# Values of the two dilated attention groups: projected in token order and re-sorted through DRAM

## The chip, the cores and the metric

The kernel runs on one core of a Trainium2 chip. The metric is the device time of one execution, in microseconds, as a median of several runs; less is better. The core has a matrix engine (TensorE, PE in the profile; its weight loads are listed apart as PEld), VectorE (DVE), ScalarE (ACT), GpSimd (POOL) and SyncE (SP), which here only issues transfers. Each engine works through its own queue in order. All operands of the matrix products are split into a high and a low part, and three products (high x high, high x low, low x high) stand for one product in full precision.

## The reference

One decoder layer over 1024 tokens of 1024 features: token mixing, a norm, a mixture of experts, a second norm. Token mixing projects the input once and hands the columns to three mixers. The one that matters here is the dilated mixer, with three groups of four heads of 64, of dilation 1, 4 and 16:

```python
def to_sub(t):
    return t.reshape(Bsz, Ls, dil, H, hd).transpose(0, 2, 1, 3, 4).reshape(Bsz * dil, Ls, H, hd)
qs, ks, vs = to_sub(q), to_sub(k), to_sub(v)
s = banded_logits(qs[:, :, :, None], ks, bias[:, None], steps)
...
o = jnp.einsum('bnhgqk,bnkhd->bnqhgd', (e / l).astype(v.dtype), band_blocks(vs, n))
```

So in a group of dilation d a token attends to tokens of its own residue class modulo d, and queries, keys and values are put in the order of the classes first. The outputs of the three groups are merged with weights from their softmax denominators. Beside it run a sliding-window mixer and a latent-attention mixer, and the output projection joins all three.

## The kernel before, in words

The part up to the routing is written as tasks. A task (line 170) is a few matrix products with the steps of other engines behind them, with estimated costs. The class Order (line 196) holds lists of tasks, the streams, in the order of the string STREAMS (line 55), and issues, one after another, the task or step that could start first by its estimates; among nearly equal ones, the earlier stream wins. Within a stream the order is fixed. Buffers are tokens: a task takes them by name when it is issued ("mm" for six PSUM banks, "ph" for four staging tiles, "v" for one large tile of values, "qk" for six query and key tiles), and gives them back after its products or steps. Stream P holds the projections, Q the scores and softmax, T the transposes of the probabilities, V the products with the values.

The projection is a list of units (line 875). A unit "cols" (cols_tasks, line 571; qk_tasks, line 607) makes 128 columns of queries or keys with the weights stationary and 512 tokens moving. A unit "v" (v_tasks, line 626) makes values key-major: x is stationary (128 features x 128 tokens), the weights move (256 columns for groups 1 and 2, 416 for group 0, which takes the values of the sliding window and the shared latent key along). Per block of 128 tokens it runs 8 feature tiles x 3 products = 24 matmuls, in two tasks. For groups 1 and 2 the block is a block of the order by residue classes, so its 128 tokens lie 4 or 8 apart in the tile of x (dilation 16 is run as 8, with every second distance masked out):

```python
                r, m = divmod(b, npc)
                sl = slice(m * P * dil + r, (m + 1) * P * dil, dil)
```

The result goes from PSUM by two steps, a cast on ACT and a subtraction on DVE (split2, line 370), straight into the tile of values "vB1" or "vB2" in its place [128 keys, block, pair, (high low low high), 64]. There is one buffer "v" for the values of all groups: a group's values can be made only when the products of the group before have read theirs.

Weights are loaded by SP in chunks of 256 KB into three raw buffers up to two units ahead (wload, line 514), and split by ACT and DVE in steps that every projection task carries (wsteps, line 523), with at most eight split chunks alive.

The order in stream P is: three latent units, then the values of group 1 mixed piece by piece with the latent keys and values (which are staged in "ph" tiles and stored to DRAM, mla_units, line 1240), then the first queries of group 1 mixed with the latent rotary part and latent queries, then keys and queries of group 1, and then for group 2 queries, keys, values, queries, keys, and the same for group 0. The attention of a group (banded, line 682) runs beside it as streams Q, T and V. The products with the values start with line 803. Outputs and statistics of groups 1 and 2 are written to DRAM by POOL (lines 999, 1062 to 1069), and so are the bias tables (row_tasks, line 462), which SP loads back (line 494).

Of the kernel before, what the change touches and what calls it, by code (L numbers as in the profile page):

```python
# [20 lines left out]
P = 128  # L21
# [33 lines left out]
STREAMS = 'VTGRLQPlE'  # L55
# [114 lines left out]
class Task:  # L170
    """Matrix products that belong together, with the work of the other engines that follows them.

    fn: a generator issues the products up to its first yield, then one step of post at a time; a plain
    function issues everything at once.  pe and post: weights of the work on the engines ("T": a transfer),
    which steer the order of issue: for a generator a list of steps (engine, weight[, step it follows]), for
    a function a list of chains of them.  alloc, free: named buffers that the task takes, and gives back
    after its products ("pe"), after a step of its post work ("at": number of steps -> buffers) or after all of it.
    """
# [10 lines left out]
class Buf:  # L189
    """A buffer of a kind, taken by one task and given back by another."""  # L190
# [5 lines left out]
class Order:  # L196
    """Issues tasks of several streams, and the steps of each, by the time at which they could start."""
# [12 lines left out]
    def take(self, kind):  # L210
        """The slot of the next buffer of this kind that the task at hand has taken."""
        return self.task.got[kind].pop(0)
# [86 lines left out]
    def run(self, streams):  # L299
        """streams: lists of tasks, the ones to prefer first."""  # L300
# [22 lines left out]
class MixedPool:  # L323
    """A pool whose tags have their own numbers of buffers."""
# [16 lines left out]
class K:  # L341
# [13 lines left out]
    def buf(self, kind, shape, dt, name):  # L355
        """A tile in the buffer of this kind that the task at hand has taken."""
        pool = {"mm": self.ps, "o": self.ps, "qk": self.qk, "ot": self.ob, "sq": self.pp}[kind]
        return pool.tile(shape, dt, name=name, tag="%s%d" % (kind, self.ord.take(kind)))

    def split(self, h, l, src, scale=None):  # L360
        """src = h + l (times scale), both exactly what a one-pass product reads."""
        nc = self.nc
        if scale is None:
            nc.scalar.copy(h, src)
            nc.vector.tensor_tensor(l, src, h.bitcast(F32), ALU.subtract)
        else:
            nc.scalar.activation(h, src, AF.Copy, scale=scale)
            nc.vector.scalar_tensor_tensor(l, src, scale, h.bitcast(F32), ALU.mult, ALU.subtract)

    def split2(self, h, l, src, scale=None, low=None):  # L370
        """The two steps of a split."""
# [11 lines left out]
    def mm3(self, out, st, mv, start, stop, **kw):  # L383
        """out += st.T @ mv for operands split as (high, low)."""
# [5 lines left out]
    # ---------------------------------------------------------------- set up  # L390
    def setup(self):
# [14 lines left out]
        self.d_v = dt("d_v", [8, P, 2, 512])  # L406
        self.d_kr = dt("d_kr", [2, 32, T])
# [11 lines left out]
    def startup(self):  # L419
        """Loads and splits x, with the first weights; returns stand-ins for when each part is there."""  # L420
# [41 lines left out]
    def row_tasks(self, g):  # L462
        """Per head -bias over the distance, +BIG where masked, replicated so that a sheared read is a table."""
# [33 lines left out]
    # ------------------------------------------------------- input projections  # L497
    def weights_of(self, unit):
        """The unit's weights in chunks of up to 2 KB: (source, shape, gains)."""
# [23 lines left out]
    def wsteps(self, u):  # L523
        """Splits the next weights of the units after u, as far as their buffers are free; then loads ahead."""
# [46 lines left out]
    def cols_tasks(self, u, unit, begin, evac, alloc=(), post=None, first=False, deps=()):  # L571
        """128 columns of the projection, d-major.  begin(): takes the destination; evac(half, psum)."""
# [34 lines left out]
    def qk_tasks(self, u, unit, cell, bufs):  # L607
        """q or k of two heads, split, tokens ordered by residue class; cell receives (high, low)."""
# [17 lines left out]
    def v_tasks(self, u, unit, begin, dests, alloc):  # L626
        """v, key-major: per 128-key block [pair, (H L | L H), 64] into dests() (column, pairs, tile)."""
        nc = self.nc
        _, key, dil = unit
        n = VCOLS[key]  # L630
        per = 2 if n == 256 else 1
        npc = 8 // dil if dil > 1 else 8
# [3 lines left out]
        def piece(b, part):  # L636
            if dil == 1:
                sl = slice(b * P, (b + 1) * P)
            else:
                r, m = divmod(b, npc)  # L640
                sl = slice(m * P * dil + r, (m + 1) * P * dil, dil)

            def fn():
                if b == 0 and part == 0:
                    begin()
# [10 lines left out]
                if part == 1:  # L656
# [11 lines left out]
        for b in range(8):  # L668
            for part in range(2):
# [3 lines left out]
                post = post + [("A", 0.48), ("D", 0.6)]  # L673
                if part == 0:
                    mm = Buf("mm")
                tasks.append(Task(piece(b, part), pe, post,
                                  alloc=([mm] if part == 0 else []) + (list(alloc) if b + part == 0 else []),
                                  free=[mm] if part else ()))
        return tasks

    # --------------------------------------------------------- banded attention
    def banded(self, name, q, k, v, tb, heads, chain, negm, l, init, out, deps, ends, ot):
        """Attention of the two heads of a tile over chains of 128-query blocks; out(bank, psum).

        q, k, v, tb, negm, l: functions, called when issued.  Returns tasks for the three streams;
        ends: (buffers given back by the last scores, by the last products)."""
# [5 lines left out]
        for b0 in range(0, 8, 2):  # L692
# [41 lines left out]
            for js in (ready[:2], ready[2:]):  # L734
# [5 lines left out]
                for h in range(2):  # L740
# [14 lines left out]
                    # the score tiles of the step before are no longer read  # L755
# [45 lines left out]
    def pv(self, out, v, p, first):  # L801
        """The halves of out add up to += v.T @ p.  v: ([a | b], high), a and b high and low or reversed; p: (high, low)."""
# [3 lines left out]
    def head_of(self, v, h):  # L806
        """([a | b], high) of a head of [keys, 4, 64]."""
        return v[:, 2 * h:2 * h + 2, :].rearrange("p i d -> p (i d)"), v[:, 3 * h]

    def unfold(self, dst, ps, h):  # L810
        """Adds up the halves of a bank of outputs of head h of a pair, to its tokens; two steps."""
# [8 lines left out]
    def spread_tasks(self, name, f, hf, use, deps, free, post=(), ps_tag="mm"):  # L820
        """Factors f() [token, block, 2 heads] of four blocks as a psum tile [2 heads x 64, 512 tokens]: use(it)."""
# [24 lines left out]
    # ----------------------------------------------------------- all mixers  # L846
    def phase_attention(self):
# [29 lines left out]
        for gi, (g, dil) in enumerate(((1, 4), (2, 8), (0, 1))):  # L877
# [4 lines left out]
            if g == 1:  # L882
                units[6 + 1] = u[0]
                u = [u[1]] + u[3:]
            units += u
# [12 lines left out]
        cells, st, tabs, vt = {}, {}, {}, {}  # L898
# [4 lines left out]
        def mixed(a, b):  # L903
            """a with b spread over it."""
            return [t for i, x in enumerate(a) for t in b[i * len(b) // len(a):(i + 1) * len(b) // len(a)] + [x]]

        for ui, u in enumerate(units):
# [6 lines left out]
            elif u[0] == "v":  # L914
# [9 lines left out]
                tk = self.v_tasks(ui, u, begin, dests, ["v", "va"] if nm == "B0" else ["v"])  # L924
                if nm == "B1":
                    early["v"] = list(tk)
                else:
                    Pt += tk
                last["v" + nm] = tk[-1]
                if nm == "B0":  # L930
# [76 lines left out]
        # sliding window with sinks  # L1007
# [32 lines left out]
        mix_end = V[-1]  # L1040
        return Pt, Q, TT, V, L, krt

    def scale_tasks(self, nm, cell, f, deps, dst, ot):
        """The outputs of a pair times its factors, and away."""
# [27 lines left out]
    def merge_tasks(self, pr, cell, st, deps, ot):  # L1072
        """The three groups' outputs weighted by exp(m_g - M) / sum."""
# [44 lines left out]
    def latent_unit(self, ui, u, name, n, lat, first, final):  # L1118
        """Compressed q or kv, normalised (the gains go into the weights), split, d-major."""
# [82 lines left out]
    def key_rope_tasks(self, kr, dep):  # L1202
        """The shared decoupled key, rotated token-major, then d-major and split."""
# [35 lines left out]
    # ------------------------------------------------------ latent attention  # L1239
    def mla_units(self, u, which, lat):  # L1240
        """Keys, queries, values of latent attention from the compressed ones, split, into DRAM."""
# [23 lines left out]
        if which == "v":  # L1265
# [19 lines left out]
            # the compressed keys and values are no longer read  # L1285
# [59 lines left out]
    def mla_open(self):  # L1345
        """Takes over from the projections."""
# [38 lines left out]
    def kq_load(self, n):  # L1385
        """Keys and queries of head n: [96, (k high, k low, q high, q low), tokens]."""
# [12 lines left out]
    def mla_tasks(self, deps, tr):  # L1399
        """Tasks of the pairs of heads."""  # L1400
# [20 lines left out]
    def dense(self, n, qp, ld, vt, tr, cell):  # L1421
        """Causal attention of a head for the query blocks 2 qp and 2 qp + 1."""
# [111 lines left out]
    # ------------------------------------ output projection, norm, routing  # L1534
    def wo_tasks(self, part, deps):
        """Weights of the output projection, four tiles of input rows, split."""
# [22 lines left out]
    def part_tasks(self, deps):  # L1559
        """alpha x + the part of the output projection that comes from the banded mixers."""  # L1560
# [51 lines left out]
    def out_tasks(self, qdeps, deps, wdeps, pend):  # L1612
        """qdeps: all scores of latent attention; deps: all of latent attention; wdeps: the weights."""
# [201 lines left out]
    def place_tasks(self, b, m, deps, c_, cell):  # L1815
        """Experts of the tokens of m blocks from b on, and the tokens' places there."""
# [92 lines left out]
    def slot_parts(self, pool, b, n=0, eng=None, nb=5):  # L1909
        """One-hot positions, and (2 token + k + 1) at the expert, of the tokens of block b."""  # L1910
# [14 lines left out]
    def slot_index(self, tabps, idx, tok):  # L1925
        """Row 2 token + k of the outputs and token of each slot; -1 where the slot is free."""
# [14 lines left out]
    def gates(self):  # L1941
        """Softmax over the chosen two, times the group's probability."""
# [15 lines left out]
    def phase_mixers(self):  # L1958
        """All mixers, output projection, norm and routing, as streams of tasks."""
        self.wos = {}  # L1960
        Pt, Q, TT, V, L, krt = self.phase_attention()
# [6 lines left out]
        m = dict(E=E, V=[V + V2], R=R, T=[TT + T2], Q=[Q + Q2], L=[L], P=[Pt + [tr] + part + Y], l=[ld, pl, wl, xl], G=G)  # L1968
        self.ord.run([s for k in STREAMS for s in m[k]])

    # --------------------------------------------------------------- experts
# [10 lines left out]
    def chunk(self, shape, i, nm):  # L1982
        """Buffer i for a chunk of weights."""
# [426 lines left out]
```

## Time and profile before

| what | value |
|---|---|
| median of three runs | 1147.3 us |
| the three runs | 1146.27, 1147.3, 1148.0 us |
| span of the profiled execution | 1146.1 us |
| mean granted TensorE clock in it | 0.957 |
| PE busy, PEld busy | 1045.4 us, 877.4 us |
| DVE, ACT, POOL busy | 768.1, 690.1, 205.7 us |
| moved by DMA | 222.65 MB, 194 GB/s on the mean |

The page gives the span, from the first to the last instruction, and no other time for the profiled execution; the runs' times lie about 1 us above it. Rows of a view of instructions read: line, engine, operation, output tile <- input tiles, shape, count, then busy time in us and the mean of one in ns, then the idle time before them with what ended it. Rows of the timeline read: start and duration in us, engine, line, operation, tiles; idle time before it stands in brackets. Records of neighbouring matmuls overlap, so the pace of PE is read from the distance of their starts. Rows by stage read: from:to in us, length, then busy time and number of instructions of PE, PEld, DVE, ACT and POOL, the granted clock, the share of DMA time and GB/s. The number behind a DMA's size is the median time from issue to landing. The value projections have the output tile psv_B, the attention outputs o_B, scores S_B, transposed probabilities pt_B; the numbers of groups and buffers are left out of the names.

### The profile page before, as it was taken

What the parts mean: (1) busy time and instruction counts of PE and PEld (TensorE: products, weight loads), DVE (VectorE), ACT (ScalarE), POOL (GpSimd) and SP (SyncE); (2) the same over time, 40 slices, a digit from 0 to 9 for tenths busy, and PEclk for the clock granted to TensorE, in tenths of its full rate; (3) what the DMA queues carried; (4) which work ended last, traced back from release to release, by engine and by line L of the source; (5) the groups of instructions that cost most, each with busy time, mean ns of one, the idle gap of its engine ahead of it and who ended that gap; (6) DMA issues with size and microseconds to landing.
All of it is one profiled execution on the core that took longest, in us unless ns stands there. A gap on an engine that the chain in (4) does not pass through costs nothing. (4 is left out here: it accounts for less than half of the span.)

```text
span 1146.1 us, 16350 instructions
## 1 busy us (share of the span) xinstructions
PE 1045.4 (91%) x5611; PEld 877.4 (77%) x5611; DVE 768.1 (67%) x1623; ACT 690.1 (60%) x1442; POOL 205.7 (18%) x219
## 2 busy tenths in 40 slices
PE   7999999999999999889999988948999999999941
PEld 5898778899879888779888867747788777777710
DVE  4443645523443566787877647787899999999758
ACT  4323255422543465687956534457999888888754
POOL 1000000200110011000310123453233222221126
PEclk9999999999989999999999989878999999999976
DMA  7135452200250311947555286447999999999273
GB/s 261 51 140 188 172 175 83 86 10 30 72 132 1 97 45 49 262 109 215 154 155 143 79 285 229 142 184 271 370 379 381 396 377 382 376 379 366 96 314 135
DMA packets 67382, 222.65 MB, mean 194 GB/s; under 512 B 12532, under 2 KB 20148, under 8 KB 53728
## 3 DMA queue, kind: packets, MB, share of 16 engines
q1 hardware_dynamic: 53328, 187.98, 46.5%
q0 software_dynamic: 13968, 33.60, 8.4%
q8 instruction: 45, 0.74, 0.3%
q14 instruction: 41, 0.34, 0.1%
HBM read 187.62 MB, written 53.82 MB: 211 GB/s over the span
## 5 line engine op out<-in xcount | busy, mean ns | idle before, releaser
L2129 DVE TENSOR_TENSOR el<-er,eh 128x1024 fp32r<-128x1024 f32 x188 | 225.9, 1220 | 26.3 <-ACT eh L2127 25.5
L2127 ACT CAST eh<-er 128x1024 fp32r<-128x1024 f32 x188 | 193.7, 1057 | 2.4 <-PE gu L388 2.0
L386 PE MATMUL gu<-eh,xh 128*128 128x512 f32 x256 | 103.8, 405 | 0.0
L387 PE MATMUL gu<-el,xh 128*128 128x512 f32 x256 | 103.7, 405 | 0.0
L388 PE MATMUL gu<-eh,xl 128*128 128x512 f32 x256 | 101.0, 395 | 0.0
L386 PE MATMUL psv_B<-wh,xH 128*128 128x256 f32 (+1 forms) x192 | 73.3, 382 | 2.2 <-ACT wh L374 1.7
L387 PE MATMUL psv_B<-wl,xH 128*128 128x256 f32 (+1 forms) x192 | 74.4, 387 | 0.4 <-DVE wl L376 0.3
L388 PE MATMUL psv_B<-wh,xL 128*128 128x256 f32 (+1 forms) x192 | 74.1, 386 | 0.0
L1456 ACT ACTIVATE PC<-PC,mnC 128x512 f32<-128x512 f32 (+3 forms) x96 | 58.6, 616 | 19.9 <-DVE mnC L1450 19.7
L1973 POOL DMA_INDIRECT xg<-d_x,tok x32 | 37.6, 1174 | 150.2 <-PE gx L2144 142.9
L387 PEld LDWEIGHTS gu<-el,xh 128*128 128x128 f32 x256 | 48.1, 188 | 20.4 <-DVE el L2129 10.3
L386 PEld LDWEIGHTS psv_B<-wh,xH 128*128 128x128 f32 x192 | 54.7, 285 | 4.6 <-ACT wh L374 2.5
L717 ACT ACTIVATE P_B<-P_B,negm_B 128x128 f32<-128x128 f32 (+1 forms) x96 | 42.4, 442 | 23.2 <-DVE negm_B L713 23.0
L1978 POOL DMA_INDIRECT d_y<-y,idx x32 | 39.4, 1232 | 92.7 <-ACT y L2182 74.8
L387 PEld LDWEIGHTS psv_B<-wl,xH 128*128 128x128 f32 x192 | 54.8, 285 | 1.6 <-DVE wl L376 1.5
L376 DVE TENSOR_TENSOR vB<-psv_B,vB 128x256 fp32r<-128x256 f32 x24 | 10.2, 424 | 68.2 <-ACT vB L374 68.2
L386 PEld LDWEIGHTS gu<-eh,xh 128*128 128x128 f32 x256 | 48.1, 188 | 10.2
L388 PEld LDWEIGHTS psv_B<-wh,xL 128*128 128x128 f32 x192 | 55.2, 287 | 0.1
L388 PEld LDWEIGHTS gu<-eh,xl 128*128 128x128 f32 x256 | 48.1, 188 | 9.2
L376 DVE TENSOR_TENSOR plC<-ptC,phC 128x512 fp32r<-128x512 f32 (+1 forms) x80 | 46.7, 630 | 11.6 <-ACT phC L374 11.1
L386 PE MATMUL y<-eh,hh 128*128 128x512 f32 x128 | 53.1, 415 | 0.7 <-ACT hh L374 0.7
L374 ACT CAST vB<-psv_B 128x256 fp32r<-128x256 f32 x24 | 8.9, 372 | 72.3 <-PE psv_B L388 72.3
(432 smaller groups left out, 2987.2 us busy)
## 6 DMA issues: line engine op xcount, KB each, us to landing
er<-in_w_gu SPq DMA_DIRECT2D x63, 1024.0 KB, 15.2
er<-in_w_dn SPq DMA_DIRECT2D x32, 1024.0 KB, 13.0
wr<-in_w_qk SPq DMA_DIRECT2D x36, 256.0 KB, 3.9
fy<-d_y SPq DMA_DIRECT2D x7, 1024.0 KB, 11.7
kqs<-d_k SPq DMA_DIRECT2D x16, 256.0 KB, 11.0
kqs<-d_qn SPq DMA_DIRECT2D x16, 256.0 KB, 5.0
vC<-d_v SPq DMA_DIRECT2D x8, 512.0 KB, 9.1
xr<-in_x SPq DMA_DIRECT2D x16, 256.0 KB, 6.4
```

The lines of the kernel that those rows point to most:

```text
L374: nc.scalar.copy(h, src)
L376: (low or nc.vector).tensor_tensor(l, src, h.bitcast(F32), ALU.subtract)
L386: nc.tensor.matmul(out, st[0], mv[0], start=start, stop=False, **kw)
L387: nc.tensor.matmul(out, st[0], mv[1], start=False, stop=False, **kw)
L388: nc.tensor.matmul(out, st[1], mv[0], start=False, stop=stop, **kw)
L717: nc.scalar.activation(p[:, i, :w], p[:, i, :w], AF.Exp, bias=negm()[:, b, hh:hh + 1], scale=-1.0, accum_out=l()[:, b, hh:hh + 1])
L1456: nc.scalar.activation(pt[:, c:c + w], pt[:, c:c + w], AF.Exp, bias=mn[:, 1:2], scale=-1.0, accum_out=sm["l"][:, b, n, i:i + 1])
L1973: self.nc.gpsimd.indirect_dma_start(out=xg, out_offset=None, in_=self.d_x1, in_offset=bass.IndirectOffsetOnAxis(ap=tok.bitcast(U32), axis= ...
L1978: return self.nc.gpsimd.indirect_dma_start(out=self.d_y, out_offset=bass.IndirectOffsetOnAxis(ap=idx.bitcast(U32), axis=0), in_=y, in_offs ...
L2127: nc.scalar.copy(hi[:, s], t[:, s])
L2129: nc.vector.tensor_tensor(lo[:, s], t[:, s], hi[:, s].bitcast(F32), ALU.subtract)
```

## The change

The values of groups 1 and 2 are now projected in blocks of 128 consecutive tokens, as those of group 0 already were. The split goes to a staging tile out of the four "ph" tiles, and SP stores it as 128 rows of 2 KB to a new DRAM tensor. When all eight blocks of a group are stored and the buffer "v" is free, POOL loads the values back, one DMA for each residue class (4 for group 1, 8 for group 2), with every dil-th row. This load is a task of a new stream N, placed ahead of P. The products with the values depend on it. The values of group 2 move ahead of that group's first queries and keys in stream P; the projection of groups 1 and 2 takes no "v" buffer any more, and the first task of group 0's values depends on group 2's load. The rest of the diff removes comments.

```diff
-STREAMS = 'VTGRLQPlE'
+STREAMS = 'VTGRLQNPlE'
...
+        self.d_vb = dt("d_vb", [2, T, 512])
...
         def piece(b, part):
-            if dil == 1:
-                sl = slice(b * P, (b + 1) * P)
-            else:
-                r, m = divmod(b, npc)
-                sl = slice(m * P * dil + r, (m + 1) * P * dil, dil)
+            sl = slice(b * P, (b + 1) * P)
...
                 yield
-                if part == 1:
+                if part == 1 and not dests:
+                    t = self.pp.tile([P, 2, 4, HD], F32R, name="vs_%s_%d" % (key, b), tag="ph")
+                    s = ps[:, :256].rearrange("p (r h d) -> p r h d", r=2, h=2)
+                    yield from self.split2(t[:, :, 0::3, :], t[:, :, 1:3, :], s)
+                    nc.sync.dma_start(self.d_vb[int(key[1]) - 1, sl], t.bitcast(F32).rearrange("p r h d -> p (r h d)"))
+                elif part == 1:
                     for c0, pairs, t in dests():
...
+                if part and not dests:
+                    post = post + [("T", 2.5)]
+                stage = ["ph"] if part and not dests else []
...
                 tasks.append(Task(piece(b, part), pe, post,
-                                  alloc=([mm] if part == 0 else []) + (list(alloc) if b + part == 0 else []),
-                                  free=[mm] if part else ()))
+                                  alloc=([mm] if part == 0 else []) + (list(alloc) if b + part == 0 else []) + stage,
+                                  free=([mm] if part else []) + stage))
...
+    def dilated_v(self, g, dil, deps):
+
+        def load():
+            t = self.vt["B%d" % g] = self.vp.tile([P, 8, 2, 4, HD], F32R, name="vB%d" % g, tag="v")
+            n = 8 // dil
+            src = self.d_vb[g - 1].rearrange("(m p r) c -> p r m c", m=n, r=dil)
+            for r in range(dil):
+                self.nc.gpsimd.dma_start(t[:, r * n:(r + 1) * n].bitcast(F32).rearrange("p m r h d -> p m (r h d)"),
+                                         src[:, r])
+
+        return Task(load, 0, [[("G", 4.0), ("T", 6.0)]], deps=deps, alloc=["v"])
...
+            elif g == 2:
+                u = [u[2]] + u[:2] + u[3:]
             units += u
...
-                tk = self.v_tasks(ui, u, begin, dests, ["v", "va"] if nm == "B0" else ["v"])
-                if nm == "B1":
-                    early["v"] = list(tk)
+                if nm != "B0":
+                    tk = self.v_tasks(ui, u, None, None, [])
+                    last["v" + nm] = self.dilated_v(int(nm[1]), u[2], tk[1::2])
+                    if nm == "B1":
+                        early["v"] = list(tk)
+                    else:
+                        Pt += tk
                 else:
+                    tk = self.v_tasks(ui, u, begin, dests, ["v", "va"])
+                    tk[0].deps = [last["vB2"]]
                     Pt += tk
-                last["v" + nm] = tk[-1]
-                if nm == "B0":
+                    last["v" + nm] = tk[-1]
...
-        m = dict(E=E, V=[V + V2], R=R, T=[TT + T2], Q=[Q + Q2], L=[L], P=[Pt + [tr] + part + Y], l=[ld, pl, wl, xl], G=G)
+        m = dict(E=E, V=[V + V2], R=R, T=[TT + T2], Q=[Q + Q2], L=[L], N=[vl], P=[Pt + [tr] + part + Y], l=[ld, pl, wl, xl], G=G)
```

More of the change, by code (lines that the diff above doesn't have):

```diff
@@ L628, in v_tasks @@
         nc = self.nc
-        _, key, dil = unit
+        key = unit[1]
         n = VCOLS[key]
         per = 2 if n == 256 else 1
-        npc = 8 // dil if dil > 1 else 8
         tasks = []
@@ L636, in piece @@
         def piece(b, part):
-            if dil == 1:
-                sl = slice(b * P, (b + 1) * P)
-            else:
-                r, m = divmod(b, npc)
-                sl = slice(m * P * dil + r, (m + 1) * P * dil, dil)
+            sl = slice(b * P, (b + 1) * P)
             def fn():
-                if b == 0 and part == 0:
+                if b == 0 and part == 0 and begin:
                     begin()
@@ L897, in phase_attention @@
         L = []
-        cells, st, tabs, vt = {}, {}, {}, {}
+        cells, st, tabs = {}, {}, {}
+        vt = self.vt = {}
         lat = {}
@@ L1039, in phase_attention @@
             V += self.scale_tasks("A%d" % j, cell, lambda f=f: f, [ft] + v[-2:], j, ot)
-        mix_end = V[-1]
-        return Pt, Q, TT, V, L, krt
+        return Pt, Q, TT, V, L, krt, [last["vB1"], last["vB2"]]
     def scale_tasks(self, nm, cell, f, deps, dst, ot):
@@ L1960, in phase_mixers @@
         self.wos = {}
-        Pt, Q, TT, V, L, krt = self.phase_attention()
+        Pt, Q, TT, V, L, krt, vl = self.phase_attention()
         tr = Task(self.mla_open, 0, deps=[Pt[-1]] + L)
```

## The prediction

> **What bounds the kernel now.** I read the page first, then the busy time by stage, then the groups of instructions by line and shape, and last the timeline of TensorE, where the intervals between matmuls stand.
>
> ```profile
> span 1146.1 us, 16350 instructions
> PE   7999999999999999889999988948999999999941
> ```
>
> The span is 1146.1 us, and the median of the three runs is 1147.3, so about 1.2 us lie around the span. PE is in use nearly everywhere. But a busy PE says little here, since neighbouring matmuls overlap in the records. What counts is whether PE ever waits, and how far apart its matmuls start. For that I cut out the stages in which the two dilated groups' values (tile psv_B, 128x256) are made:
>
> ```profile
> core 0: us, PE busy (x) PEld busy (x) DVE busy (x) ACT busy (x) POOL busy (x), PEclk, DMA share, GB/s
> 51.70:108.60 56.90, 56.56 (x257) 54.38 (x256) 20.96 (x45) 16.02 (x37) 0.00 (x0) 1.00 0.40 151
> 140.00:150.00 10.00, 10.00 (x45) 7.73 (x44) 4.37 (x7) 4.26 (x8) 0.51 (x1) 1.00 1.01 369
> 188.80:221.00 32.20, 32.07 (x201) 26.59 (x201) 19.28 (x54) 20.20 (x55) 5.89 (x10) 1.00 0.35 108
> 221.00:271.60 50.60, 50.60 (x249) 50.20 (x249) 9.81 (x46) 11.79 (x46) 2.25 (x3) 1.00 0.05 12
> ```
>
> In the first stage (values of group 1, between pieces of the latent keys and values) and in the last (values of group 2) PE has no gap, its weight loads (PEld) are in use for 96% and 99% of the time, DVE and ACT for less than half, and DMA is at 151 and 12 GB/s. So these two stages are bound by PE, and inside PE by the loads of the stationary operand. The row of 140 to 150 is there for what DMA can do: 369 GB/s.
>
> ```profile
> L388 PEld LDWEIGHTS psv_B<-wh,xL 128*128 128x128 f32 x64 | 21.1, 330 | 0.0
> L388 PEld LDWEIGHTS mv<-wh,cl 128*128 128x128 f32 x8 | 1.5, 188 | 0.4
> L387 PE MATMUL psv_B<-wl,xH 128*128 128x256 f32 x128 | 51.2, 400 | 0.0
> ```
>
> The first two rows are of the stage 45 to 110 and of one size, 128x128 f32. Loading x for a residue class, every fourth token, takes 330 ns; loading adjacent columns takes 188. The Trainium skill ("TensorE: Matmul & The Clock Gate", LDWEIGHTS) lets the time of a load depend on its number of columns alone; the two rows differ at the same number of columns, so here the measurement decides. The third row is of the whole run: 128 matmuls for each of the three products of a split pair, so 384 strided loads in all, 192 for each group.
>
> **The change, part by part.** *The stride goes.* The intervals before:
>
> ```profile
> 98.28 0.28 PE L386 MATMUL psv_B<-wh,xH 128*128 128x256 f32 x1
> 100.97 0.40 PE L386 MATMUL mv<-wh,ch 128*128 128x512 f32 x1
> 101.67 0.28 PE L386 MATMUL psv_B<-wh,xH 128*128 128x256 f32 x1
> ...
> 241.34 0.40 PE L386 MATMUL psv_B<-wh,xH 128*128 128x256 f32 x1
> 251.46 0.40 PE L386 MATMUL psv_B<-wh,xH 128*128 128x256 f32 x1
> ```
>
> Group 1 comes in 16 runs of 12 matmuls, and a run takes 100.97 - 98.28 = 2.69 us. In group 2 the two rows are 42 matmuls apart: 10.12 / 42 = 0.241 us each. The profile has no 128x256 matmul whose stationary operand is x in adjacent columns. Its neighbours are these:
>
> ```profile
> 355.06 0.35 PE L387 MATMUL psv_B<-wl,xH 128*128 128x416 f32 x1
> 361.03 0.35 PE L386 MATMUL psv_B<-wh,xH 128*128 128x416 f32 x1
> ...
> 423.93 0.28 PE L803 MATMUL o_B<-ph_B,vB 128*128 128x256 f32 x1
> 424.40 0.28 PE L803 MATMUL o_B<-ph_B,vB 128*128 128x256 f32 x1
> ...
> 420.31 1.03 PE L746 MATMUL pt_B<-ident,P_B 128*128 128x128 f32 x8
> 421.11 0.48 PE L386 MATMUL ps_kA<-xH,wh 128*128 128x512 f32 x1
> ```
>
> The first pair is the same helper on the third value unit, with adjacent tokens but 416 columns: 32 intervals in 5.97 us, 0.187 each. That is an upper bound, since 256 columns cannot take longer than 416. The second pair has 256 columns; 4 intervals in 0.47 us, 0.1175 each, but every second load there has only 64 columns. The third has full 128x128 loads under 128 columns: 8 in 0.80 us, 0.10 each, the lower bound. I take 0.1175, which has the right number of columns; the third pair shows that full loads keep up with it. With it a run of group 1 takes 12 x 0.1175 = 1.41 us, so 16 x (2.69 - 1.41) = 20.5 us go. In group 2, 192 x (0.241 - 0.1175) = 23.7 us go. Together 44.2. By the lower bound it is 16 x 1.49 + 192 x 0.141 = 50.9, by the upper one 16 x 0.45 + 192 x 0.054 = 17.6.
>
> The Trainium skill (same page, Back-to-back issue gap) gives 256 / 2.4 + 2.5 = 109 ns between such matmuls; by that estimate 47.4 us would go. For 416 columns the same formula says 176 ns where the rows above show 187, so I stay with the rows.
>
> *The split now ends in a staging tile and a store.* ACT and DVE do the same two steps per block as before. New are 16 stores of 256 KB on SP's queue, 8 in each group, from a staging tile in the ring "ph" of four, which the latent tiles and the attention's probabilities use too. The nearest stores, and the split as it stands now:
>
> ```profile
> d_k<-k_0l SPq DMA_DIRECT2D x4, 256.0 KB, 2.0
> d_v<-vt0l SPq DMA_DIRECT2D x1, 256.0 KB, 2.2
> ...
> 58.01 0.37 ACT L374 CAST vB<-psv_B 128x256 fp32r<-128x256 f32 x1 [2.10 <-PE psv_B L388]
> 58.87 0.41 DVE L376 TENSOR_TENSOR vB<-psv_B,vB 128x256 fp32r<-128x256 f32 x1
> 106.40 0.32 SPq L1261 DMA_DIRECT2D d_v<-vt6h  x1
> ```
>
> A staging tile is held from the cast to the landing: 1.27 us to the end of the subtraction, 0.32 for SP to issue, 2.2 to land, 3.8 in all. In group 1's stage a value block comes with two latent tasks of 3 matmuls. Those take 101.67 - 100.97 = 0.70 us each, so 3 slots of the ring are taken every 2 x (1.41 + 0.70) = 4.2 us, and a slot is wanted again after 4 x 4.2 / 3 = 5.6 us. 3.8 fits. DMA carried 56.9 us x 151 GB/s = 8.6 MB in this stage; with 2.1 MB of stores over about 36 us that is 297 GB/s, below the 369 seen. So I cost the stores at nothing, with the ring's 1.8 us of slack as the cover. Behind each store on SP stand the loads of the next weights; they wait at most for the subtraction in front of the store, 0.41 us, and are issued two units ahead. If that cover is gone, PE waits as in these rows, about 2 us each time:
>
> ```profile
> 110.81 0.50 PE L386 MATMUL ps_qB<-xH,wh 128*128 128x512 f32 x1 [2.20 <-ACT wh L374]
> 335.58 0.45 PE L386 MATMUL psv_B<-wh,xH 128*128 128x416 f32 x1 [1.68 <-ACT wh L374]
> ```
>
> Both stand at the start of a unit whose weights are not split yet. They stay, since the number of live weights is not changed. I allow for one more of the kind: +2 us.
>
> *The values are loaded back*, 4 DMAs of 512 KB for group 1 and 8 of 256 KB for group 2, on POOL's queue. Nearest rows:
>
> ```profile
> 183.42 0.55 POOL L999 DMA_DIRECT2D d_ob<-oB  x1 [26.28 <-DVE oB L817]
> 216.69 2.87 POOL L1062 DMA_DIRECT2D d_stat<-negm_B  x4
> d_ob<-oB POOLq DMA_DIRECT2D x4, 512.0 KB, 3.9
> rt<-in_c_ropet POOLq DMA_DIRECT2D x1, 1024.0 KB, 5.1
> ...
> 134.91 0.50 POOL L472 CAST oh<-ohr 33x384 fp32r<-33x384 f32 x1 [110.60 <-DVE qr11l L376]
> L803 PEld LDWEIGHTS o_B<-ph_B,vB x100: 186/188/192, 164.7 to 436.9; 128*128 128x128 f32 x100
> 143.00:154.00 11.00, 10.96 (x48) 8.93 (x48) 0.69 (x1) 0.59 (x1) 1.00 0.95 334
> ```
>
> An issue costs 0.55 to 0.72 us, so 8 cost 4.4 to 5.7; with the landing of the last store (2.2) before and 3.9 to 5.1 behind, a load takes 10 to 13 us. Group 1's values are wanted first at 164.7, in the new time at about 144; now they are ready at about 51.7 + 36 + 10 = 98. POOL's own next step there is the cast of the first bias table, which waits for the latents until 134.91; should the load be queued behind it, it is there at 134.9 - 20.5 + 13 = 127, still early, and the other way round the cast waits for nothing that is late. Group 2's projection no longer waits for the single buffer "v", it fills PE beside group 1's second attention; only its load waits for that buffer. Between that moment and the first use lie the q and k units of group 2's first pair, 11 us of PE each (last row, one k unit, 48 matmuls), so 22 us cover 13. POOL has the statistics of group 1 in front or behind, 2.87 us for one of two such groups of four; this fits too. What is late next: PE itself, with the 128x512 units.
>
> *The sum.* 1146.1 - 44.2 + 2 = 1103.9 of span, with 1.2 around it: 1105 us.
>
> **The rivals.** *The load of group 2's values ends on the path.* The new order gives PE group 2's values as filler in the stage 188.8 to 221, and takes them away from its own attention, so if the planner lets the attention reach its products before the load has landed, PE waits for the whole chain. Against it stand the 22 us above. Price: 13 us, and a spell of lowered clock behind it. What such a spell costs is seen here:
>
> ```profile
> 108.60:142.60 34.00, 31.22 (x121) 24.34 (x120) 21.15 (x33) 11.35 (x20) 0.50 (x1) 0.90 0.48 172
> ```
>
> The row begins with the 2.20 us wait above, and its mean granted clock (PEclk) of 0.90 over 34 us is worth 3.4 us. So 1105 + 13 + 3.4 = 1121.
>
> *Nothing gained.* If the strided load were not what spaces the matmuls, they would stay at 2.69 / 12 = 0.224 to 0.241 us and the stores would come on top: 1147.3 + 2 = 1149. That is where the skill's rule on loads would lead. Against it: 416 columns go at 0.187.
>
> *Slower: the staging ring.* If landing is slow, the four slots set the pace of group 1's stage: 24 uses / 4 x hold. With the landing of a loaded stage,
>
> ```profile
> er<-in_w_gu SPq DMA_DIRECT2D x63, 1024.0 KB, 15.2
> kqs<-d_k SPq DMA_DIRECT2D x16, 256.0 KB, 11.0
> ```
>
> 15.2 us, the hold is 16.8 and the stage 101 us in place of 34, which gives 1105 + 67 = 1172. It decides against the change from a hold of (34 + 42) / 6 = 12.7 us, a landing of 11.1; the second row is just under that. Against it: stores in this very stage land in 2.0 to 2.2, and the stage's DMA stays below 369 GB/s.
>
> **How the numbers follow.** The forecast, 1105, has 0.74 with its own spread of 1097 (lower bound of the interval, 1146.1 - 50.9 + 1.2 = 1096.4) to 1112 (some ring or weight waits of 2 us); the load on the path 0.17; nothing gained 0.04; the ring 0.05. The range takes in the first two, 1097 to 1121; left out are the last two cases and the tails, among them the interval of 0.187, which would give 1132. Differences under 0.2%, 2.3 us, cannot be told from none. Faster: 0.74 + 0.17 = 0.91; same: 0.04 (1149 lies 1.7 us off); slower: 0.05.
>
> **What would show it.** Right: psv_B's loads in groups 1 and 2 near 188 ns, intervals near 0.12 us, group 1's stage some 36 us long, the group of 2's attention with no PE wait on the load, the stores landing in under 4 us. Wrong: idle time of ACT before the staging casts ended by a DMA (ring); idle time of PE before group 2's first products ended by the load of the values, with a dip in PEclk behind it (load on the path); intervals still above 0.2 (nothing gained).

## The result and the profile after

The changed kernel takes 1106.42 us (median of five runs, 1101.59 to 1107.22) beside 1146.27 us for the kernel before (median of five as well). The ratio is 0.964, with a 95% interval of 0.9617 to 0.9663, so about 40 us are gone. The profiled execution of the changed kernel is the fastest of the five, 1101.59 us. Its span of 1099.9 us is 46.2 us below that of before; three of the other four runs have spans of 1104.7 to 1105.5. So the traces show where the 46 us of two single executions went, and the medians say what to expect: 40.

The stages that answer to those of the prediction, of the changed kernel (from:to, length, busy time of PE, PEld, DVE, ACT and POOL, granted clock, DMA share, GB/s):

```profile
span 1099.9 us, 16432 instructions
core 0: us, PE busy (x) PEld busy (x) DVE busy (x) ACT busy (x) POOL busy (x), PEclk, DMA share, GB/s
51.50:87.90 36.40, 36.34 (x257) 33.46 (x256) 20.71 (x45) 15.91 (x37) 0.00 (x0) 1.00 0.73 272
165.40:198.80 33.40, 33.12 (x298) 31.99 (x298) 17.92 (x54) 18.98 (x55) 6.32 (x10) 1.00 0.38 120
```

The first stage holds the same work as 51.7 to 108.6 before, 257 matmuls, in 36.4 us instead of 56.9: 20.5 less. The second is group 2's values, which now run beside group 1's second attention. PE has no gap of note in either, as before; it only goes faster. The groups of loads and matmuls, and the timeline inside the two groups:

```profile
L388 PEld LDWEIGHTS psv_B<-wh,xL 128*128 128x128 f32 x64 | 12.1, 190 | 0.0
L387 PE MATMUL psv_B<-wl,xH 128*128 128x256 f32 x128 | 36.1, 282 | 0.0
...
85.83 0.28 PE L387 MATMUL psv_B<-wl,xH 128*128 128x256 f32 x1
86.90 0.28 PE L387 MATMUL psv_B<-wl,xH 128*128 128x256 f32 x1
...
193.82 0.28 PE L387 MATMUL psv_B<-wl,xH 128*128 128x256 f32 x1
195.98 0.28 PE L387 MATMUL psv_B<-wl,xH 128*128 128x256 f32 x1
```

The loads are at 190 ns, from 330. Nine intervals in 1.07 us and 18 in 2.16 are 0.119 and 0.120 us, from 0.224 and 0.241. Two landmarks bound the rest: the first keys of group 1, and the first matmul of group 0's values. First the kernel before, then the changed one:

```profile
143.04 0.49 PE L386 MATMUL ps_kB<-xH,wh 128*128 128x512 f32 x1
329.53 0.35 PE L386 MATMUL psv_B<-wh,xH 128*128 128x416 f32 x1
```

```profile
120.45 0.49 PE L386 MATMUL ps_kB<-xH,wh 128*128 128x512 f32 x1
283.62 0.35 PE L386 MATMUL psv_B<-wh,xH 128*128 128x416 f32 x1
```

Between the landmarks lie 186.5 us before and 163.2 after: 23.3 less, for group 2. From the second landmark to the end it is 816.6 and 816.3. Most of what is left of the 46.2 lies between the end of group 1's stage and the first landmark, 1.9 us. The granted clock there is 0.90 over 34.4 us before and 0.95 over 32.6 us after, which is worth 3.4 and 1.6 us; the difference, 1.8, is that rest.

The new transfers of the changed kernel: the loads of group 1 (x4) and of group 2 (x8) on POOL, the DMA rows with the time from issue to landing, and the first use of group 2's values:

```profile
91.08 2.88 POOL L694 DMA_DIRECT2D vB<-d_vb  x4 [67.68 <-DMA d_v<-vt7h]
203.00 4.28 POOL L694 DMA_DIRECT2D vB<-d_vb  x8 [0.67 <-DMA wr<-in_w_qk]
d_vb<-vs_B SPq DMA_DIRECT2D x16, 256.0 KB, 3.9
vB<-d_vb POOLq DMA_DIRECT2D x8, 256.0 KB, 6.2
229.21 0.22 PE L821 MATMUL o_B<-ph_B,vB 128*128 128x128 f32 x1
```

Group 2's load ends at about 203.0 + 4.3 + 6.2 = 213.5, some 16 us before its first use.

### The profile page after: what moved, and what is told of

It reads as the page before. It is cut to its first block, busy times and chain, and to the rows that moved or that the text cites. A ratio compares the mean times of both kernels' runs of the same rounds, so it can differ in the third digit from the quotient of the medians.

```text
span 1099.9 us, 16432 instructions
## 1 busy us (share of the span) xinstructions
PE 998.8 (91%) x5611; PEld 831.0 (76%) x5611; DVE 767.5 (70%) x1623; ACT 690.2 (63%) x1442; POOL 214.7 (20%) x231
## 5 line engine op out<-in xcount | busy, mean ns | idle before, releaser
L387 PEld LDWEIGHTS gu<-el,xh 128*128 128x128 f32 x256 | 48.4, 189 | 20.5 <-DVE el L2154 10.6
L386 PE MATMUL psv_B<-wh,xH 128*128 128x256 f32 (+1 forms) x192 | 60.4, 315 | 2.9 <-ACT wh L374 2.9
L387 PE MATMUL psv_B<-wl,xH 128*128 128x256 f32 (+1 forms) x192 | 59.5, 310 | 0.4 <-DVE wl L376 0.4
L388 PE MATMUL psv_B<-wh,xL 128*128 128x256 f32 (+1 forms) x192 | 59.1, 308 | 0.0
L387 PE MATMUL y<-el,hh 128*128 128x512 f32 x128 | 50.6, 395 | 0.0
L388 PE MATMUL y<-eh,hl 128*128 128x512 f32 x128 | 50.4, 394 | 0.0
L374 ACT CAST phC<-ptC 128x512 fp32r<-128x512 f32 (+1 forms) x80 | 38.8, 549 | 13.3 <-PE ptC L1504 13.0
L376 DVE TENSOR_TENSOR xl<-gx,xh 128x512 fp32r<-128x512 f32 x64 | 43.6, 684 | 3.0 <-issue 2.3
L2207 ACT COPY y<-y 128x512 f32<-128x512 f32 x64 | 37.6, 588 | 11.9 <-PE y L388 9.6
```

The costliest lines, as they stand in the source:

```text
L376: (low or nc.vector).tensor_tensor(l, src, h.bitcast(F32), ALU.subtract)
L386: nc.tensor.matmul(out, st[0], mv[0], start=start, stop=False, **kw)
L387: nc.tensor.matmul(out, st[0], mv[1], start=False, stop=False, **kw)
L388: nc.tensor.matmul(out, st[1], mv[0], start=False, stop=stop, **kw)
L2207: nc.scalar.copy(y[e][:, s], ps)
```

## The experiments

The theory: the gain is the pace of the loads of x alone, and the trip through DRAM is hidden. The rivals: the new order, with the projection of group 2 freed from the buffer "v", gains something by itself; the trip costs something that a larger gain hides. Each run stands beside runs of the kernel before on the same chip, whose medians were 1145.7 to 1146.8 us.

**Only group 1 changed.** Group 2 keeps the strided loads, the direct write and its old place:

```diff
+            if dests and dil > 1:
+                r, m = divmod(b, 8 // dil)
+                sl = slice(m * P * dil + r, (m + 1) * P * dil, dil)
+            else:
+                sl = slice(b * P, (b + 1) * P)
...
-            elif g == 2:
-                u = [u[2]] + u[:2] + u[3:]
```

> Only group 1 is made from adjacent tokens and goes through DRAM; group 2 stays as before, in its place and order. If the pace of the strided loads is all there is, 20.5 of the 44 us go: about 1126 us beside a before of 1146, with matmul intervals of 0.12 us in group 1 and 0.241 in group 2. If a good part of the gain comes from group 2's values no longer waiting for the single buffer of values, less than half of it shows here, and this run stays above 1130.

Measured: 1125.1 us, ratio 0.984 (0.981 to 0.987). The loads of this run, first in the stage of group 1, then in that of group 2:

```profile
L388 PEld LDWEIGHTS psv_B<-wh,xL 128*128 128x128 f32 x64 | 12.1, 190 | 0.0
...
L388 PEld LDWEIGHTS psv_B<-wh,xL 128*128 128x128 f32 x62 | 21.0, 338 | 0.0
```

By the medians 21.0 of the 40 us belong to group 1, and the rest, 18.7, to group 2. By the ratios it is 18 us (15 to 22) for group 1 and 23 for group 2, so the times alone give this split to some 4 us only. The time came out at the number worked out from the pace alone.

**The whole change with strided loads.** Staging, stores, loads, order and streams are those of the changed kernel, and only the blocks are residue classes again:

```diff
-            sl = slice(b * P, (b + 1) * P)
+            if not dests:
+                r, m = divmod(b, 8 // dil)
+                sl = slice(m * P * dil + r, (m + 1) * P * dil, dil)
+            else:
+                sl = slice(b * P, (b + 1) * P)
...
-            src = self.d_vb[g - 1].rearrange("(m p r) c -> p r m c", m=n, r=dil)
+            src = self.d_vb[g - 1].rearrange("(r m p) c -> p r m c", m=n, r=dil)
```

> Everything of the change but the adjacent tokens: the blocks are those of the residue classes again (strided loads of x), still staged, stored, loaded back (now in order) and moved ahead of group 2's queries. If the stride is the whole cause, the time goes back to that of before, 1146 to 1149 us, with loads of 330 ns. If the new order or the freed buffer gains by itself, it is under 1140.

Measured: 1146.63 us, ratio 1.0015 (0.9997 to 1.0033). The loads of this run, group by group of instructions, first in the stage of group 1, then in that of group 2:

```profile
L388 PEld LDWEIGHTS psv_B<-wh,xL 128*128 128x128 f32 x64 | 21.1, 330 | 0.0
...
L388 PEld LDWEIGHTS psv_B<-wh,xL 128*128 128x128 f32 x64 | 21.6, 338 | 0.0
```

With the stride back, the whole gain is gone. The order, the freed buffer and the trip through DRAM together change nothing that can be measured.

**Adjacent tokens and nothing else.** The kernel before, without the sorting of the values:

```diff
-            if dil == 1:
-                sl = slice(b * P, (b + 1) * P)
-            else:
-                r, m = divmod(b, npc)
-                sl = slice(m * P * dil + r, (m + 1) * P * dil, dil)
+            sl = slice(b * P, (b + 1) * P)
```

> The kernel before, with adjacent tokens and nothing else: the values go straight into their tile, in the wrong order, so the sorting of the values is left out. This is the gain without the trip through DRAM. If the trip is hidden, the time is that of the changed kernel, 1104 to 1108 us. If the trip costs something, it is faster than the changed kernel by that, at most 2 us by the prediction's allowance, up to 16 by the rival of the load on the path. If the new order itself helps, this run is slower than the changed kernel, 1110 or more.

Measured: 1104.83 us, ratio 0.9657 (0.963 to 0.9684), against 0.964 (0.9617 to 0.9663) for the changed kernel. The intervals overlap: the trip of 16 stores and 12 loads, with the order that comes with it, costs nothing that can be told apart. This run and the one before it have trip and order both or neither, so a cost of the one could still hide behind a gain of the other. Against that stand runs further down: with the stores doubled, or group 2's loads doubled, the time stays where it was.

**Strides 1 to 8.** The kernel before, with block b of group 2 from tokens b + 1 apart:

```diff
+            elif dil == 8:
+                sl = slice(0, (b + 1) * P, b + 1)
```

> The kernel before, with block b of group 2 made from tokens b+1 apart (strides 1 to 8), so group 2's values are other tokens'. Only the loads and intervals by block are read. If what counts is that at least two values fall in one line of 16 bytes (four values), strides 1 and 2 give loads near 188 ns and intervals near 0.12 us, 4 and above 330 to 340 ns and 0.233 to 0.241, and 3 lies between. If the cost grows with the distance itself, it rises step by step up to stride 8.

It is one execution, of which only the rows are read. The loads by block, from five windows, for strides 1, 2, 3, 4 and 8 (the number behind the comma is the mean in ns):

```profile
L388 PEld LDWEIGHTS psv_B<-wh,xL 128*128 128x128 f32 x8 | 1.5, 192 | 0.0
...
L388 PEld LDWEIGHTS psv_B<-wh,xL 128*128 128x128 f32 x8 | 1.6, 196 | 0.0
...
L388 PEld LDWEIGHTS psv_B<-wh,xL 128*128 128x128 f32 x7 | 1.8, 261 | 0.0
...
L388 PEld LDWEIGHTS psv_B<-wh,xL 128*128 128x128 f32 x8 | 2.7, 333 | 0.0
...
L388 PEld LDWEIGHTS psv_B<-wh,xL 128*128 128x128 f32 x7 | 2.4, 338 | 0.0
```

The median distances of the matmuls' starts in these blocks are 0.120, 0.120, 0.174, 0.235 and 0.242 us. A stride of 2 is free, 3 lies between, and from 4 on the cost is full and no longer grows with the distance (5 to 7: 318 to 331 ns). The Trainium skill ("SBUF — State Buffer", the note on cachelines) says that lines are 16 bytes and that two accesses must fall in one line to be fast. The blocks agree with that: at stride 2 two f32 values share a line, and from 4 on each has one to itself. At stride 3 half of the values share a line; an estimate from the blocks at 1 and 4 is then (192 + 333) / 2 = 262 ns, and the block shows 261. The same note puts the free stride at four f32 values; by these rows it is two.

**Two and four stores.** Every staging tile is stored twice, or four times, first to tensors that nobody reads:

```diff
-                    nc.sync.dma_start(self.d_vb[int(key[1]) - 1, sl], ...)
+                    for dst in [*self.d_vx, self.d_vb]:
+                        nc.sync.dma_start(dst[int(key[1]) - 1, sl], ...)
```

> The changed kernel with every store of a staging tile made twice, the first time to a DRAM tensor that nobody reads. In group 1's stage DMA then moves 8.6 + 4.2 = 12.8 MB in about 36 us, 356 GB/s, just under the 369 seen. If the four staging tiles have slack, as the prediction costs it (a slot held 3.8 us, wanted again after 5.6), the time stays within 4 us of the changed kernel, 1105 to 1111. If the ring is already at its limit, a hold that grows by the second store and its transfer (about 1 us or more) shows in all 16 blocks, 1115 or more.

> The same with four stores of every staging tile. Group 1's stage then has 8.6 + 8.4 = 17 MB to move, 46 us at 369 GB/s in place of some 36, and in group 2's stage the ring is shared with the attention. If the ring and DMA set the pace once their slack is used up, the time rises by 10 to 15 us, to 1116 to 1121, with ACT waiting for a staging tile. If stores are never on the path, it stays at 1106.

Measured: 1106.73 us with two (ratio 0.9648, 0.9627 to 0.9669), 1115.05 with four (0.9735, 0.9703 to 0.9768). Twice the stores cost nothing that the time shows, four times cost 9 us, just under the first of the two cases expected. Where these go, in the run with four: the stage of group 1's values and the 10 us behind it, the first matmul after it, what ACT waited for in staging tiles, and the end of ACT's queue before that matmul:

```profile
50.80:87.90 37.10, 36.70 (x258) 33.56 (x256) 18.38 (x40) 14.10 (x32) 0.00 (x0) 1.00 0.88 333
87.90:98.00 10.10, 0.13 (x2) 0.11 (x1) 3.51 (x9) 3.92 (x10) 0.00 (x0) 0.60 1.05 406
97.89 0.80 PE L386 MATMUL ps_qB<-xH,wh 128*128 128x512 f32 x1 [9.97 <-ACT wh L374]
ACT vt3h L1303 <- DMA d_vb<-vs_B: 4.2, 1, 4.2
ACT vt5h L1303 <- DMA d_vb<-vs_B: 2.9, 1, 2.9
ACT vt7h L1303 <- DMA d_vb<-vs_B: 2.8, 1, 2.8
ACT k_1h L374 <- DMA d_vb<-vs_B: 1.3, 1, 1.3
...
92.51 0.37 ACT L374 CAST vs_B<-psv_B 128x256 fp32r<-128x256 f32 x1 [0.67 <-DMA d_v<-vt4h]
95.73 0.37 ACT L1303 CAST vt7h<-mv 128x256 fp32r<-128x256 f32 x1 [2.85 <-DMA d_vb<-vs_B]
97.21 1.15 ACT L374 CAST wh<-wr 128x512 fp32r<-128x512 f32 x2
```

PE passes the stage nearly unslowed, 37.1 us for 36.4. ACT does wait for staging tiles whose store of values has not landed, four times and 11.2 us in all, but PE runs ahead into the free PSUM banks: its stage ends at 87.9, and ACT casts the last value block at 92.5. The debt falls due behind the stage. DMA works off its backlog at 406 GB/s, ACT casts the last latent tile at 95.73, where the changed kernel does so at 88.03, and the first queries wait 9.97 us for weights whose split stands behind that cast in ACT's queue, where the changed kernel waits 2.20. ACT is 7.7 us later, and PE waits 7.8 us longer. With two stores the same waits stand between: 5.2 us of ACT for staging tiles and 4.08 us of PE, beside 1.3 and 2.20 in the changed kernel. So DMA gave out first; the ring handed its delay to ACT, and ACT's queue handed it to PE one unit later.

**One unit of cover for the load.** Group 2's values between its first queries and its first keys:

```diff
-                u = [u[2]] + u[:2] + u[3:]
+                u = [u[0], u[2], u[1]] + u[3:]
```

> The changed kernel with group 2's values between its first queries and its first keys, so that 11 us of projections instead of 22 lie between the last store and the first scores. If the load of 10 to 13 us is hidden with room to spare (the second pair's queries and keys can fill PE while the products wait), the time stays at 1105 to 1109. If the two units are the cover that keeps the load off the path, the products of group 2 wait and the time rises towards the rival's 1121.

Measured: 1104.81 us (0.9629, 0.9597 to 0.9661). The load and the first use in this run:

```profile
214.37 4.29 POOL L694 DMA_DIRECT2D vB<-d_vb  x8 [12.25 <-DMA wr<-in_w_qk]
229.79 0.22 PE L821 MATMUL o_B<-ph_B,vB 128*128 128x128 f32 x1
```

The load starts 11 us later, and the first use stays where it was. Half the cover is enough.

**The load twice, four times, ten times.** To find where the cover ends:

```diff
-            for r in range(dil):
+            for r in list(range(dil)) * (10 if g == 2 else 1):
```

> The changed kernel with group 2's values loaded back twice, each second load of a residue class behind the first. In the changed kernel's profile the load is issued from 203.0 us, a round of eight takes about 4.3 us to issue and 6.2 to land, and the first product with these values starts at 229.2. Two rounds end at about 220 to 224: if the load has 16 us of slack, the time does not move, 1103 to 1109. If the cover was only just enough, it rises by up to 10.

> The same with four rounds, which end at about 235 to 245, 6 to 16 us behind the first use. If the rival's mechanism is real once the cover is used up, PE waits there for the load and the time rises by that wait and a spell of lowered clock, to 1112 to 1125. If PE has other work to put in its place, it stays at 1103 to 1109.

> The changed kernel with group 2's values loaded back ten times in a row. With four rounds the last issue was at 228.3, and a round after the first two took about 8 us, so ten rounds end near 275 to 280, 40 us or more behind the first use at about 231. If PE's order is fixed and the products stand in it at that place, PE waits 40 us or more less whatever projections it passes meanwhile, and the time is 1140 or above. If the planner's order leaves the products room, much less of it shows.

Measured: 1104.25 us with two, 1103.73 with four, 1136.26 with ten (ratio 0.9911, 0.9881 to 0.9941). With four I had expected the load to end behind its first use. The last issues and the first use in that run:

```profile
222.92 5.93 POOL L694 DMA_DIRECT2D vB<-d_vb  x9 [0.23 <-DMA vB<-d_vb]
231.22 0.22 PE L821 MATMUL o_B<-ph_B,vB 128*128 128x128 f32 x1
```

The last load went out at 228.3 and, with the 6.6 us that a load of this run took, landed at about 235. So the load did end some 4 us behind the first use, and still PE has no wait: of the two cases that were expected, the first, with the wait, did not come. With ten, the first use, the stage around it, and the last loads that POOL issued:

```profile
262.88 0.45 PE L821 MATMUL o_B<-ph_B,vB 128*128 128x128 f32 x1 [31.25 <-DMA vB<-d_vb]
235.00:262.00 27.00, 0.00 (x0) 0.00 (x0) 0.00 (x0) 0.00 (x0) 19.67 (x38) 0.53 1.02 384
261.28 3.19 POOL L694 DMA_DIRECT2D vB<-d_vb  x6 [2.42 <-issue]
```

PE stands still for 31.25 us at exactly the place that the rival named, with nothing else on any engine but POOL. The time rises by 32 us over the run with four, to less than the 1140 expected. One reason is in the last row: when the first product starts, at 262.88, POOL is still issuing the last round's loads, until 264.5. So this product did not wait for the whole round; that each waits for the load of its own residue class alone also fits the run with four. The other reason is that the rounds ended earlier than the 275 to 280 expected. So the mechanism is real, but the threshold lies between four and ten rounds.

**The PSUM bank given back on paper before the store:**

```diff
-                                  free=([mm] if part else []) + stage))
+                                  free=([mm] if part and not stage else []) + stage,
+                                  free_at={2: [mm]} if stage else ()))
```

> The changed kernel, in which the planner counts a value block's PSUM bank as free after the subtraction instead of after the store. Only the order of issue can change. If PE is dense because enough work is always ready, nothing changes: 1103 to 1108. If the bank held on paper through the store delays the projections, this run is faster than 1103.

Measured: 1104.24 us (0.964, 0.9615 to 0.9665), the same as the changed kernel.

**Weights split two units ahead.** An attempt at the waits that stay in the changed kernel:

```diff
-        if not (self.w_loaded and self.w_live < 8 and self.w_loaded[0][0] <= u + 1):
+        if not (self.w_loaded and self.w_live < 8 and self.w_loaded[0][0] <= u + 2):
```

> Not a part of the change: the changed kernel, with the splitting of weights allowed two units ahead instead of one. It aims at the waits at the start of units that stay in the changed kernel's profile (2.20 us for the first queries of group 1, at a clock that then drops). If these waits come from weights that are loaded but not split yet, 4 to 8 us go: 1098 to 1102. If the eight live chunks are the limit and not the rule, nothing changes: 1104 to 1108.

Measured: 1110.15 us (0.9682, 0.9665 to 0.9698), slower than the changed kernel. The first matmul of the unit that used to wait, and the longest waits of the stage behind it (total, times, longest):

```profile
90.99 0.40 PE L386 MATMUL ps_qB<-xH,wh 128*128 128x512 f32 x1
ACT wh L374 <- DMA wr<-in_w_qk: 17.8, 5, 7.8
PE mpq L386 <- DVE t L1334: 4.8, 1, 4.8
PE S_B L386 <- DVE negm_B L731: 3.7, 1, 3.7
```

The wait aimed at is gone: no idle time stands at 90.99, where the changed kernel has 2.20 us. But the splits now reach the head of ACT's queue before their weights have landed, 17.8 us in five waits, and everything behind them on ACT and DVE is late, until PE waits 4.8 and 3.7 us in other places. This expectation fell. None of the runs beats the changed kernel by more than their intervals.

## Why the prediction was right

**What bounds the stage.** Right: PE, and in it the loads. Restoring the stride alone takes back all of the gain, and removing it alone gives all of it. The rule on the time of a load that the prediction quotes from the Trainium skill, by which nothing would have been gained, is contradicted by the strides run: 192 to 338 ns at the same number of columns.

**The pace.** 0.1175 us was taken, 0.119 to 0.120 was measured. Group 1 was put at 20.5 us and gave 20.5 between the two profiles, and 21.0 as the median of the run with group 1 alone. Group 2 was put at 23.7; it gave 23.3 between the landmarks, and 18.7 as the difference of two medians, which is uncertain by some 4 us. The 109 ns that the prediction quotes from the Trainium skill ("TensorE: Matmul & The Clock Gate", Back-to-back issue gap) is given there for a matmul by itself, without its load. With the loads, the runs here show 0.119 to 0.120 us.

**The stores.** Costed at nothing, rightly, but with too small a hold. The only store whose landing the changed kernel's profile shows took 3.9 us and not 2.2; in the run with one unit of cover, whose stage of group 1 is the same, the eight stores took 2.2 to 4.0. And a store can stand behind loads of weights on SP, which the working has only the other way round. Of the changed kernel:

```profile
75.12 1.32 SPq L519 DMA_DIRECT2D wr<-in_w_qk  x2
76.55 0.37 SPq L658 DMA_DIRECT2D d_vb<-vs_B  x1
80.51 0.37 ACT L1301 CAST vt3h<-mv 128x256 fp32r<-128x256 f32 x1 [1.31 <-DMA d_vb<-vs_B]
```

This slot was held from its cast at 74.58 to 80.51, 5.9 us and more than the 5.6 of the prediction, and ACT waited 1.31 us for it. So the slack I named was used up once. That it did not show in the time, nor with twice the stores, has another reason: PE runs ahead into free PSUM banks while ACT waits. DMA was put at 297 GB/s in this stage and was at 272.

**The load.** 10 to 13 us were expected, with the landing of the last store in it. Counted like that, from the issue of the last store (88.19 and 199.8), group 1's load took 91.08 + 2.88 + 8.6 - 88.19 = 14.4 us and group 2's 213.5 - 199.8 = 13.7, a little more than the upper end. It was covered, as said. The chance of 0.17 for this rival looks too high beside the runs: half the cover is enough, and four rounds of the load show no wait.

**The 2 us for one more weight wait.** There was no third wait; the two that were quoted stayed, as these rows of the changed kernel show, one of them longer:

```profile
90.19 0.79 PE L386 MATMUL ps_qB<-xH,wh 128*128 128x512 f32 x1 [2.20 <-ACT wh L374]
290.06 0.46 PE L386 MATMUL psv_B<-wh,xH 128*128 128x416 f32 x1 [2.92 <-ACT wh L374]
```

The sum agrees with the median within 1.4 us, partly by luck: the profiled executions differ by 46.2 us, 4 more than I forecast, and the medians by 39.9, 2 less. Of the 4, 2 are the wait that did not come and 1.9 the stretch behind group 1's stage, which the sum left out; the two terms of the pace, 20.5 and 23.3, make 43.8 for the 44.2 forecast. Why runs of one kernel differ by 5 us is not settled here; the lengths of lowered clock in the profiles differ from run to run.

**The rival on the other side.** The ring as a price of 67 us did not come, since the stores that can be seen in this stage landed in at most 4.0 us, far from the 11.1 that it needed. But a weak form of its mechanism is there: ACT's waits for staging tiles grow from 1.3 to 5.2 and 11.2 us with one, two and four stores. What the rival had wrong is who pays. The ring never set the pace of PE in its stage; the delay went through ACT's queue and fell due at the next unit's weights.

## What to carry to other kernels

Where PE has no gap, read the loads' own durations beside the matmuls': two groups of the same size with different durations point at the layout of the operand. Sorting is then better left to a DMA that other work covers than to the load of the stationary operand, which is paid again at every matmul. And when extra traffic is added to a stage, look for its price one stage later, in the queue that fell behind, not only where it was put.

## What the hardware showed that was not expected

Loading a stationary operand of f32 at stride 2 is as fast as an adjacent one (196 ns beside 192), and stride 8 hardly slower than 4 (338 beside 333). Stores and loads together reached 406 GB/s in the run with four stores, above the 369 that I had taken from the profile of before as what DMA can do. The 369 was a mean over 10 us: from 142 to 144 us the same profile shows 405.
